# A two-layer decoder trunk on one core: halves of the convolution weights rounded behind copies of queries and probabilities, mixtures in the large pool's banks, and the order of roundings in the down projection

## The chip, the cores and the metric

One core of a Trainium2 chip runs the whole program. The metric is the device time of one execution in microseconds (us); of several runs the median is given. The engines are TensorE (PE, matrix products), VectorE (DVE), ScalarE (ACT), GpSimd (POOL) and SyncE (SP, here the issuer of nearly all DMAs). Each has its own queue of instructions and works through it in order.

## The reference, cut to what matters

512 tokens of width 1024 go through two layers. Layer 0 mixes by sliding-window attention beside a short gated convolution, layer 1 by a gated linear attention; each layer then has a gated feed-forward part with a convolution over time and a per-layer embedding gate.

```python
def _attn_conv_mixer(h, cos, sin, w_in, q_norm, k_norm, sinks, conv_w, w_out):
    b, s, _ = h.shape
    q, k, v, cb, cc, cx = _split(h @ w_in, HY_SPLITS)
    q = _apply_rope(_rms_norm(q.reshape(b, s, ATTN_Q_HEADS, HEAD_DIM), q_norm), cos, sin)
    k = _apply_rope(_rms_norm(k.reshape(b, s, ATTN_KV_HEADS, HEAD_DIM), k_norm), cos, sin)
    v = v.reshape(b, s, ATTN_KV_HEADS, HEAD_DIM)
    attn = _sliding_window_sink_attention(q, k, v, sinks)
    conv = cb * _causal_depthwise_conv(cc * cx, conv_w)
    return jnp.concatenate([attn, conv], axis=-1) @ w_out

def _conv_ffn(h, w_up, conv_w, conv_b, w_down):
    u = _causal_depthwise_conv(h @ w_up, conv_w) + conv_b
    gate, up = jnp.split(u, 2, axis=-1)
    return (jax.nn.gelu(gate, approximate=False) * up) @ w_down
...
    for i in range(DEPTH):
        j = i // 2
        h = _rms_norm(x, mix_norm[i])
        if i % 2 == 0:
            x = x + _attn_conv_mixer(h, cos, sin, hy_w_in[j], ...)
        else:
            x = x + _gla_mixer(h, gla_w_in[j], ...)
        x = x + _conv_ffn(_rms_norm(x, ffn_norm[i]), ffn_w_up[i], ffn_conv_w[i], ffn_conv_b[i], ffn_w_down[i])
        x = x + _per_layer_embedding(x, p[i], ple_norm[i], ple_w_gate[i], ple_w_proj[i])
```

The attention has 8 query heads of width 64 over 2 key heads, a window of 128 and four blocks of 128 queries. The down projection takes 2816 rows to 1024 columns.

## The kernel before, in words

**Numbers in two parts.** Every float32 operand of a large product is rounded to float32r (the high part) and the rest is kept as a second float32r tile (the low part). `cut` does it for weights: ScalarE copies `raw` to `wh` (L146), VectorE subtracts to get `wl` (L147), in pieces of 128x1024. `mm3` then makes three matmuls: high by high (L166), high by low (L167) and low by high (L168). `split` does the same for activations (L109 on ScalarE, L110 on VectorE). `weights` loads a piece of 1024 KB by SP into one of two `raw` buffers and cuts it.

**Banks.** TensorE writes to two pools of four banks each: `ps`, the large pool of this text, for the sums of long products, and `pa`, for transposes, scores and part products.

**The mixer of layer 0.** Queries, keys and values are made first. Then the four attention blocks run, between the products of the convolution: `conv_in` multiplies the tokens by 256 columns of the weights x, c or b, as two products of 24 matmuls of 128x512 each (the first with the first 128 columns, the second with the other 128), for two groups `j2` of columns. For a block `t`, `query` scales and turns the queries by position, `query_turned` transposes them on TensorE and copies them with ScalarE to `qT` (L547), `scores` makes query by key (L611, a `pa` bank for each pair), masks with VectorE and takes the exponentials with ScalarE, `probs` scales them (L652 on ScalarE), transposes them (L658) and copies them to `pT` (L664 on VectorE, L666 on ScalarE), and `mix` multiplies them by the values into one bank and splits the result to the operands `b0`, `b1` (L109, L110). The code writes these calls out in a fixed order, interleaved with `conv_w` (load and round 256 columns). Here a scheduler sets the order of the instructions on each engine, from that order and its own estimates; `tc.issue_after(x)` keeps an instruction behind `x`, which in the orders below shows only on the engine of that instruction.

**The down projection.** `down` goes through a list `plan` of 16 steps in the order written, for four units `u` of 256 columns. A step is a plain product (its matmuls are L166 to L168 into `ps`), and four of them have a fifth entry `s`, the number of a unit of 256x256 blocks that is multiplied with seven products instead of eight: `seven` (matmuls L886 to L888), a generator that is advanced by `next(g)` between the matmuls of the plain step. Its part sums are copied from bank to bank by ScalarE: L897, L907 and, last, L911 (`turned_over`), without which the next product in that bank can't go on. `cut_blocks` rounds a unit's weights (L833 on ScalarE, L834 on VectorE), and L857, L858 and L865 form differences of weight blocks on VectorE. `todo` lists the roundings of coming steps, and `pump(1)` issues what has come due. `settled(ends)` adds the finished banks of a unit to the residual `xT` (`add`, L1194) and starts the next norm (`finish`, whose squares and scaled copies are L276, L285 and L1321). TensorE's order in `down` is that of the code; the other engines' is the scheduler's.

```python
                    next(g)
                    cut_done(s)
                    pump(1)
                    steps(3, 4)
                    pump(1)
                    settled(ends)
```

Of the kernel before, what the change touches and what calls it, by code (L numbers as in the profile page):

```python
# [14 lines left out]
ALU = mybir.AluOpType  # L15
# [3 lines left out]
P = 128  # L19
# [3 lines left out]
ND = D // P  # L23
# [33 lines left out]
class Kernel:  # L57
# [369 lines left out]
    def mixer0(self):  # L427
        nc, a, tc = self.nc, self.a, self.tc
        with tc.tile_pool(name="m0", bufs=1) as mp:
            w_in = a["hy_w_in"][0].rearrange("(k p) n -> p k n", p=P)  # L430
# [111 lines left out]
            def turned(x, dst, copy):  # L542
                pst = self.pa()
                for g in range(4):
                    pairv = x[:, 2 * g : 2 * g + 2, :].rearrange("p a b -> p (a b)")
                    nc.tensor.transpose(pst[:, g * P : (g + 1) * P], pairv, self.ident)
                copy(dst, pst)  # L547


            kT = self.sp.tile([P, S], F32, tag="acc", name="kT", bufs=1)  # L550
# [38 lines left out]

            def query_turned(t, qn):  # L590
                qT = mp.tile([P, 4, P], F32, tag="qT", name=f"qT{t}", bufs=4)
                turned(qn, qT.rearrange("p a b -> p (a b)"), nc.scalar.copy)
                qTs.append(qT)

            ss, dens = {}, {}
            ya = [self.pair(self.fp, "b0", "b1") for _ in range(4)]

            def scores(t):
# [40 lines left out]
                nc.vector.reciprocal(den, den)  # L639
                ss[t], dens[t] = s, den  # L640

            pTs, copied = {}, {}

            def probs(t):

# [21 lines left out]

            def mix(t):

                po = self.pa()  # L670
                n = 2 if t else 1
                for g in range(2):
                    for c in range(n):
                        v = vs[t - 1 + c] if t else vs[0]
                        nc.tensor.matmul(
                            po[64 * g : 64 * g + 64, :], v[:, g * HD : (g + 1) * HD],
                            pTs[t][:, c, 4 * g : 4 * g + 4, :].rearrange("p a b -> p (a b)"),
                            start=c == 0, stop=c == n - 1,
                        )
                for j in range(4):  # L680
                    cols = slice(t * P, (t + 1) * P)
                    self.split((ya[j][0][:, cols], ya[j][1][:, cols]), po[:, j * P : (j + 1) * P])


            yc = [None] * 4
# [5 lines left out]
            def conv_w(nme, j2):  # L691
                c0 = starts[nme] + 256 * j2
                return self.weights(w_in[:, :, c0 : c0 + 256], ND, 256)

            def conv_in(nme, w):
                for c in range(2):
# [23 lines left out]
            def conv_out(j2, cs=(0, 1)):  # L720
                for c in cs:
                    xs, y = pre[c]
                    nc.vector.tensor_tensor(xs, pss["b", c], R, ALU.mult)
                    nc.vector.tensor_tensor(y, y, xs, ALU.mult)
                    hl = self.pair(self.fp, "b0", "b1")
                    self.split(hl, y)
                    yc[2 * j2 + c] = hl


            w = conv_w("x", 0)  # L730
# [11 lines left out]
            query_turned(1, qn1)  # L742
            scores(0)
            conv_in("c", w)
            w = conv_w("b", 0)
            conv_taps(0)
            qn3 = query(3)
            query_turned(2, qn2)
            probs(0)
            scores(1)  # L750
            conv_in("b", w)
            w = conv_w("x", 1)
            conv_out(0, (0,))
            query_turned(3, qn3)
            mix(0)
            probs(1)
            with tc.issue_after(copied[1, 0]):
                conv_out(0, (1,))
            scores(2)
            conv_in("x", w)  # L760
            w = conv_w("c", 1)
            mix(1)
            probs(2)
            scores(3)
            conv_in("c", w)
            w = conv_w("b", 1)
            conv_taps(1)
            mix(2)
            probs(3)
# [337 lines left out]
    def down(self, i, acts, forms, both, work, finish):  # L1107
# [83 lines left out]
                f()  # L1191

        def add(m, ps):
            nc.vector.tensor_tensor(self.xT[m], self.xT[m], ps, ALU.add)  # L1194

        due = [2 if u < blocked else 1 for u in range(4)]
        block_left = blocked
# [3 lines left out]
        with tc.manual_schedule(engines={ET.PE}):  # L1201
# [4 lines left out]
            for t, (u, name, k0, k1, s) in enumerate(plan):  # L1206
# [25 lines left out]
                if s is None:  # L1232
                    steps(0, k1 - k0)
                    settled(ends)
                    pump(1)
                    pend()
                    if work:
                        work.pop(0)()
                        if not work:
                            load_inner(inner.pop(0))  # L1240
                else:
                    g = gens[s]
                    steps(0, 1)
                    next(g)
                    steps(1, 2)
                    next(g)
                    steps(2, 3)
                    next(g)
                    cut_done(s)
                    pump(1)  # L1250
                    steps(3, 4)
                    pump(1)
                    settled(ends)
                    X, Y, V = next(g)
                    pump(1)
                    x = self.xT[2 * s + 1].rearrange("p (u t) -> p u t", u=2)
                    nc.vector.tensor_tensor(x, x, V.unsqueeze(1).to_broadcast([P, 2, H]), ALU.add)
                    if s == 3:
                        banks[3] = [X, Y]
                    else:  # L1260
                        add(2 * s, X)
                        add(2 * s + 1, Y)
                    pend()
                    due[s] -= 1
                    block_left -= 1
                    settled(False)
# [864 lines left out]
```

## Time and profile before

| | us |
|---|---|
| three runs, median (lowest to highest) | 1200.52 (1199.79 to 1200.64) |
| the profiled execution | 1201.93 |
| its span in the profile | 1200.1 |
| TensorE busy, in the span | 1191.8 |
| VectorE busy | 994.1 |
| ScalarE busy | 685.1 |

In the lines of a profile, a time stands first (us from the start of the span), then the duration, the engine, the line of the kernel, the operation, the tile that is written, an arrow and the tiles that are read, and the shape. "x16" is a group of sixteen such instructions on a row; the duration is then from the first's start to the last's end. In brackets stands the idle time of the engine before it and who ended it. A line of the list of waits has the waiting engine, tile and line, the engine, tile and line that released it, the sum of the waits, their count and the mean. Matmuls are pipelined, so their records overlap: how long one takes in a row is seen from the next one's start.

### The profile page before, as it was taken

To read this page: it belongs to the slowest core of one execution; us is meant where nothing else is said; L and a number is where in the kernel's file an instruction comes from. 1 tells how busy PE (TensorE), PEld (TensorE's weight loads), DVE (VectorE), ACT (ScalarE), POOL (GpSimd) and SP (SyncE) were. 2 spreads that over 40 slices of the span, in tenths; PEclk is the share of its full clock that TensorE was granted. 3 is DMA by queue.
4 is the path that set the end of the run, shared out by engine and by line. 5 is a ranking of instruction groups with operands and counts; after the bars stand their busy time and mean duration, and the time that the engine had idled before them with its cause. 6 is when DMAs were issued, how large, how long until landed. Compare 5 with 4: busy or idle time off the path is not lost.

```text
span 1200.1 us, 17976 instructions
## 1 busy us (share of the span) xinstructions
PE 1191.8 (99%) x7121; PEld 1038.1 (87%) x7121; DVE 994.1 (83%) x1571; ACT 685.1 (57%) x1116; POOL 43.0 (4%) x64
## 2 busy tenths in 40 slices
PE   9999999999999999999999999999999999999998
PEld 8877788999899889889988988889899999889887
DVE  6786587899999996779779876687999999986895
ACT  7566465556565744566563564555555656644764
POOL 2600000000000000000100000000000000000000
PEclk9999999999999999999999999999999999999999
DMA  7221322423233343331422222323242423423601
GB/s 223 86 91 38 97 80 70 127 85 118 94 101 111 106 141 97 97 106 61 149 59 70 71 71 70 106 64 112 71 141 71 134 79 119 136 88 97 211 1 70
DMA packets 110856, 117.62 MB, mean 98 GB/s; under 512 B 2824, under 2 KB 105794, under 8 KB 110772
## 3 DMA queue, kind: packets, MB, share of 16 engines
q1 hardware_dynamic: 109936, 115.88, 29.9%
q8 instruction: 56, 0.92, 0.3%
q0 software_dynamic: 560, 0.42, 0.3%
q14 instruction: 28, 0.23, 0.1%
q10 hardware_dynamic: 276, 0.18, 0.1%
HBM read 114.37 MB, written 2.10 MB: 97 GB/s over the span
## 4 chain that ended last, share of the span: by engine, by line
PE 89%; DVE 5%; ACT 2%; issue 1%; DMA 1%; POOL 1%; SPq 0%; DVEq 0%; ACTq 0%; POOLq 0%
PE ps L166 12%; PE ps L167 12%; PE ps L168 12%; PE pa L167 7%; PE pa L166 7%; PE pa L168 7%; PE ps L886 6%; PE ps L888 6%; PE ps L887 6%; PE pa L886 2%; PE pa L888 2%; PE pa L887 2%; PE ps L1496 1%; PE ps L1495 1%; PE ps L1494 1%
## 5 line engine op out<-in xcount | busy, mean ns | idle before, releaser
L146 ACT ACTIVATE wh<-raw 128x1024 fp32r<-128x1024 f32 (+4 forms) x144 | 143.6, 998 | 112.4 <-PE ps L167 64.8
L147 DVE TENSOR_TENSOR wl<-raw,wh 128x1024 fp32r<-128x1024 f32 (+4 forms) x144 | 165.8, 1152 | 29.9 <-ACT wh L146 29.0
L833 ACT ACTIVATE wh<-raw 128x1024 fp32r<-128x1024 f32 x84 | 89.2, 1062 | 120.6 <-DVE raw L858 65.1
L946 DVE SCALAR_TENSOR_TENSOR zt<-z,vfa,zt 128x510 f32<-128x510 f32 (+1 forms) x176 | 130.9, 746 | 5.3 <-ACT zt L944 4.7
L834 DVE TENSOR_TENSOR wl<-raw,wh 128x1024 fp32r<-128x1024 f32 x84 | 102.8, 1223 | 22.5 <-ACT wh L833 22.4
L944 ACT ACTIVATE zt<-z,vfb 128x512 f32<-128x512 f32 x88 | 71.1, 810 | 21.7 <-DVE four L997 8.3
L166 PE MATMUL ps<-b,wh 128*128 128x512 f32 x192 | 76.3, 397 | 0.0
L167 PE MATMUL ps<-b,wh 128*128 128x512 f32 x192 | 75.0, 390 | 0.0
L168 PE MATMUL ps<-b,wl 128*128 128x512 f32 x192 | 74.9, 390 | 0.0
L886 PE MATMUL ps<-four,wh 128*128 128x256 f32 x256 | 71.6, 280 | 0.7 <-ACT ps L911 0.7
L888 PE MATMUL ps<-four,wl 128*128 128x256 f32 x256 | 71.0, 277 | 0.0
L887 PE MATMUL ps<-four,wh 128*128 128x256 f32 x256 | 70.8, 277 | 0.0
L167 PE MATMUL pa<-b,wh 128*128 128x512 f32 x176 | 69.0, 392 | 0.0
L167 PE MATMUL pa<-a,wh 128*128 128x512 f32 x176 | 69.0, 392 | 0.0
L166 PE MATMUL pa<-a,wh 128*128 128x512 f32 x176 | 69.0, 392 | 0.0
L166 PE MATMUL pa<-b,wh 128*128 128x512 f32 x176 | 69.0, 392 | 0.0
L168 PE MATMUL pa<-b,wl 128*128 128x512 f32 x176 | 68.5, 389 | 0.0
L168 PE MATMUL pa<-a,wl 128*128 128x512 f32 x176 | 68.4, 389 | 0.0
L886 PEld LDWEIGHTS ps<-four,wh 128*128 128x128 f32 x256 | 48.0, 188 | 3.4 <-ACT ps L911 1.6
L166 PE MATMUL ps<-a,wh 128*128 128x512 f32 x128 | 50.6, 395 | 0.0
L166 PE MATMUL ps<-uh,wh 128*128 128x512 f32 x128 | 50.3, 393 | 0.0
L167 PE MATMUL ps<-ul,wh 128*128 128x512 f32 x128 | 50.1, 391 | 0.0
(496 smaller groups left out, 3597.1 us busy)
## 6 DMA issues: line engine op xcount, KB each, us to landing
raw<-in_ffn_w_up_dram SPq DMA_DIRECT2D x44, 1024.0 KB, 5.1
raw<-in_ffn_w_down_dram SPq DMA_DIRECT2D x12, 1024.0 KB, 5.1
raw<-in_hy_w_in_dram SPq DMA_DIRECT2D x8, 1024.0 KB, 5.1
raw<-in_gla_w_in_dram SPq DMA_DIRECT2D x8, 1024.0 KB, 5.2
raw<-in_ffn_w_down_dram SPq DMA_DIRECT2D x8, 768.0 KB, 4.4
raw<-in_ple_w_gate_dram SPq DMA_DIRECT2D x6, 1024.0 KB, 5.1
raw<-in_hy_w_out_dram SPq DMA_DIRECT2D x16, 256.0 KB, 4.1
zt<-in_ffn_w_down_dram SPq DMA_DIRECT2D x8, 512.0 KB, 3.7
```

Source lines behind the costliest of these rows:

```text
L146: nc.scalar.activation(hv, v, AF.Copy)
L147: self.rest = nc.vector.tensor_tensor(lv, v, hv.bitcast(F32), ALU.subtract)
L166: mm(out, lh, rh, start=start, stop=False, **kw)
L167: mm(out, lh, rl, start=False, stop=False, **kw)
L168: return mm(out, ll, rh, start=False, stop=stop, **kw)
L833: nc.scalar.activation(h, src, AF.Copy)
L834: nc.vector.tensor_tensor(l, src, h.bitcast(F32), ALU.subtract)
L886: mm(out, wh, xh, start=first and j == 0, stop=False, **kw)
L887: mm(out, wh, xl, start=False, stop=False, **kw)
L888: mm(out, wl, xh, start=False, stop=j == ND // 2 - 1, **kw)
L944: nc.scalar.activation(y, z, AF.Identity, scale=w2[:, f : f + 1], bias=bb[:, f : f + 1])
L946: nc.vector.scalar_tensor_tensor(out=y[:, tap:], in0=z[:, : S - tap], scalar=w[:, f : f + 1], in1=y[:, tap:], op0=ALU.mult, op1=ALU.add,)
```

## The change

Three things change.

1. In the mixer, `turned` returns its copy, and `copied["q", t]` holds that of `qT`. The weights b of the first group and x, c and b of the second are no longer rounded by `conv_w` but by `conv_halves`: the same load, and then the two halves of 128 columns each with a `cut` of its own, behind an instruction that is named: b's first half behind the copy of block 1's turned queries and its second behind the second ScalarE copy of block 0's probabilities; x's behind that and behind the last split of block 0's mixture; both of c's behind block 1's second ScalarE copy of probabilities; both of the last b's behind block 2's.
2. `mix` takes its bank from `ps`, not from `pa`.
3. In `down`, in the steps that have a seven-product unit, the last matmuls of the plain step and the additions (`settled`) come ahead of the two `pump(1)`, and what the first of these issues is kept behind L911 and, where a unit ended, behind the last addition.

```diff
@@ -544,7 +544,7 @@
-                copy(dst, pst)
+                return copy(dst, pst)
@@ -589,10 +589,10 @@
-                turned(qn, qT.rearrange("p a b -> p (a b)"), nc.scalar.copy)
+                copied["q", t] = turned(qn, qT.rearrange("p a b -> p (a b)"), nc.scalar.copy).ins
@@ -667,7 +667,7 @@
-                po = self.pa()
+                po = self.ps()
@@ -679,7 +679,8 @@
-                    self.split((ya[j][0][:, cols], ya[j][1][:, cols]), po[:, j * P : (j + 1) * P])
+                    last = self.split((ya[j][0][:, cols], ya[j][1][:, cols]), po[:, j * P : (j + 1) * P])
+                mixed[t] = last[1].ins
@@ -691,6 +692,20 @@
+            def conv_halves(nme, j2, ins):
+                c0 = starts[nme] + 256 * j2
+                raw = self.raw(ND, 256)
+                nc.sync.dma_start(raw, w_in[:, :, c0 : c0 + 256])
+                ws = []
+
+                def half(ins):
+                    c = slice(len(ws) * P, len(ws) * P + P)
+                    with tc.issue_after(ins):
+                        ws.append(self.cut(raw[:, :, c], "b"))
+
+                half(ins)
+                return (lambda k, a, b: ws[a // P](k, 0, P)), half
@@ -742,28 +757,32 @@
-            w = conv_w("b", 0)
+            w, second = conv_halves("b", 0, copied["q", 1])
             conv_taps(0)
             qn3 = query(3)
             query_turned(2, qn2)
             probs(0)
+            second(copied[0, 1])
             scores(1)
             conv_in("b", w)
-            w = conv_w("x", 1)
+            w, second = conv_halves("x", 1, copied[0, 1])
             conv_out(0, (0,))
             query_turned(3, qn3)
             mix(0)
             probs(1)
             with tc.issue_after(copied[1, 0]):
                 conv_out(0, (1,))
+            second(mixed[0])
             scores(2)
             conv_in("x", w)
-            w = conv_w("c", 1)
+            w, second = conv_halves("c", 1, copied[1, 1])
+            second(copied[1, 1])
             mix(1)
             probs(2)
             scores(3)
             conv_in("c", w)
-            w = conv_w("b", 1)
+            w, second = conv_halves("b", 1, copied[2, 1])
+            second(copied[2, 1])
@@ -1191,7 +1210,7 @@
-            nc.vector.tensor_tensor(self.xT[m], self.xT[m], ps, ALU.add)
+            self.added = nc.vector.tensor_tensor(self.xT[m], self.xT[m], ps, ALU.add)
@@ -1247,10 +1266,14 @@
                     cut_done(s)
+                    steps(3, 4)
+                    settled(ends)
+                    with ExitStack() as es:
+                        es.enter_context(tc.issue_after(self.turned_over.ins))
+                        if ends:
+                            es.enter_context(tc.issue_after(self.added.ins))
+                        pump(1)
                     pump(1)
-                    steps(3, 4)
-                    pump(1)
-                    settled(ends)
```

How the instructions move: line numbers of the changed kernel are larger by up to 23 (L833 becomes L852, L834 L853, L897 L916, L907 L926, L911 L930, L1194 L1213, L1321 L1344), and buffer numbers differ. First ScalarE around block 1's turned queries, before:

```order
L146 ACTIVATE wh_808<-raw_802 128x1024
L712 ACTIVATE cy_818<-pad_813,vec_104_682 128x512
L652 ACTIVATE s_713<-s_713,den_738 128x128 x4
L146 ACTIVATE wh_966<-raw_964 128x1024
L547 COPY qT_850<-pa_851 128x512
L666 COPY pT_862<-pa_863 128x512
L666 COPY pT_862<-pa_869 128x512
```

and after:

```order
L727 ACTIVATE cy_814<-pad_809,vec_104_682 128x512
L652 ACTIVATE s_713<-s_713,den_738 128x128 x4
L547 COPY qT_846<-pa_847 128x512
L666 COPY pT_858<-pa_859 128x512
L666 COPY pT_858<-pa_865 128x512
L727 ACTIVATE cy_824<-pad_819,vec_104_682 128x512
L146 ACTIVATE wh_871<-raw_802 128x1024
L146 ACTIVATE wh_966<-raw_964 128x1024
```

`raw_802` is the load of b and `raw_964` that of x. The second half of b and the first half of x moved from ahead of the copies of `qT` and `pT` to behind them. On VectorE in the next block, before:

```order
L724 TENSOR_TENSOR cy_828<-cy_828,cxs_822 128x512
L147 TENSOR_TENSOR wl_1126<-raw_1123,wh_1125 128x1024
L664 COPY pT_1003<-pa_1010 128x512
L110 TENSOR_TENSOR b_67_549<-pa_987,b_66_548 128x128
L664 COPY pT_1003<-pa_1022 128x512
L110 TENSOR_TENSOR b_69_551<-pa_987,b_68_550 128x128
```

and after:

```order
L739 TENSOR_TENSOR cy_824<-cy_824,cxs_818 128x512
L110 TENSOR_TENSOR b_67_549<-ps_983,b_66_548 128x128
L664 COPY pT_999<-pa_1006 128x512
L110 TENSOR_TENSOR b_69_551<-ps_983,b_68_550 128x128
L664 COPY pT_999<-pa_1018 128x512
```

The rest of c's weights (`raw_1123`) left this place for one behind the masking of the scores; the mixture's splits (L110) read a `ps` bank. On ScalarE in that block, x's second half (`wh_1030`) now stands where c's first half stood, ahead of `qT`, and c's first half comes after the copies of `pT`. Last, ScalarE in the first seven-product unit of layer 0's down projection, before:

```order
L907 COPY ps_4367<-ps_4368 128x256
L146 ACTIVATE wh_4451<-raw_4299 128x1024
L911 COPY ps_4368<-ps_4367 128x256
L109 ACTIVATE wh_4461<-zt_4271 128x4x128
L109 ACTIVATE wh_4461<-zt_4273 128x4x128
L833 ACTIVATE wh_4495<-zt_4271 128x1024
L276 ACTIVATE acc_4073<-xT_103 128x512
L1321 ACTIVATE sum_5118<-xT_103,vec_104_682 128x512
L897 COPY ps_4518<-pa_4516 128x256
```

and after:

```order
L926 COPY ps_4367<-ps_4368 128x256
L930 COPY ps_4368<-ps_4367 128x256
L146 ACTIVATE wh_4459<-raw_4299 128x1024
L109 ACTIVATE wh_4463<-zt_4271 128x4x128
L109 ACTIVATE wh_4463<-zt_4273 128x4x128
L276 ACTIVATE acc_4073<-xT_103 128x512
L1344 ACTIVATE sum_5118<-xT_103,vec_104_682 128x512
L852 ACTIVATE wh_4495<-zt_4271 128x1024
L916 COPY ps_4518<-pa_4516 128x256
```

The bank copy L911 goes ahead of the rounding L146, and the two norm instructions go ahead of the unit's rounding L833. VectorE at the same place has both additions L1194 of the finished unit ahead of L147, where one stood behind L857; and the first addition of the next unit ahead of L858, where it stood behind it. The orders of POOL and of SP's DMAs are unchanged.

More of the change, by code (lines that the diff above doesn't have):

```diff
@@ L591, in query_turned @@
                 qT = mp.tile([P, 4, P], F32, tag="qT", name=f"qT{t}", bufs=4)
-                turned(qn, qT.rearrange("p a b -> p (a b)"), nc.scalar.copy)
+                copied["q", t] = turned(qn, qT.rearrange("p a b -> p (a b)"), nc.scalar.copy).ins
                 qTs.append(qT)
-            ss, dens = {}, {}
+            ss, dens, copied, mixed = {}, {}, {}, {}
             ya = [self.pair(self.fp, "b0", "b1") for _ in range(4)]
@@ L640, in scores @@
                 ss[t], dens[t] = s, den
-            pTs, copied = {}, {}
+            pTs = {}
             def probs(t):
```

## The prediction

> **What bounds the kernel now.** I read the page's engine sums first, then the waits of TensorE, then the timeline of TensorE in the stretches that the diff touches, then ScalarE and VectorE in the same stretches.
>
> ```profile
> span 1200.1 us, 17976 instructions
> PE 1191.8 (99%) x7121; PEld 1038.1 (87%) x7121; DVE 994.1 (83%) x1571; ACT 685.1 (57%) x1116; POOL 43.0 (4%) x64
> PE ps L886 <- ACT ps L911: 0.7, 1, 0.7
> PE pa L611 <- DVE pT L664: 0.5, 1, 0.5
> PE pa L611 <- DVE b L110: 0.3, 1, 0.3
> ```
>
> PE is busy 1191.8 of 1200.1 us, and the diff takes no matmul away. It can only win back gaps between matmuls. The listed waits it could touch are 0.5 and 0.3 us; the 0.7 us one is in the feed-forward of layer 1, where nothing changes. Smaller stalls hide inside "busy", since a matmul's record is longer than its turn. So I measure the step from one start to the next.
>
> ```profile
> 45.11 0.39 PE L168 MATMUL ps<-a,wl 128*128 128x512 f32 x1
> 45.34 0.39 PE L166 MATMUL ps<-a,wh 128*128 128x512 f32 x1
> 69.66 1.39 PE L658 MATMUL pa<-cf,s 128*128 128x128 f32 x8
> 70.97 2.81 PE L611 MATMUL pa<-kT,qT 64*128 64x256 f32 x16
> 73.71 0.50 PE L166 MATMUL ps<-a,wh 128*128 128x512 f32 x1
> 88.02 0.47 PE L166 MATMUL ps<-a,wh 128*128 128x512 f32 x1
> 88.94 1.99 PE L611 MATMUL pa<-kT,qT 64*128 64x256 f32 x12 [0.45 <-DVE pT L664]
> 92.26 0.50 PE L167 MATMUL ps<-a,wh 128*128 128x512 f32 x1
> 105.02 1.99 PE L658 MATMUL pa<-cf,s 128*128 128x128 f32 x16
> 106.93 2.81 PE L611 MATMUL pa<-kT,qT 64*128 64x256 f32 x16
> 109.67 0.50 PE L166 MATMUL ps<-a,wh 128*128 128x512 f32 x1
> ```
>
> A free 128x512 matmul takes 0.23 us (45.11 to 45.34). Sixteen transposes of L658 take 1.91 us (105.02 to 106.93), so eight should take 0.95; in block 1 they took 1.31 (69.66 to 70.97): 0.36 lost. Twelve score matmuls of L611 have a record of 1.99 with the tail of the last, so sixteen should take 16/12 of 1.99 less its tail of some 0.29, so 2.27 us, an estimate; blocks 1 and 3 took 2.74 (70.97 to 73.71, 106.93 to 109.67): 0.47 lost in each. Block 2 lost 0.92 − 0.23 = 0.69 ahead of the scores (88.02 to 88.94) and 3.32 − 2.27 = 1.05 in them (88.94 to 92.26). Together 3.0 us: all that the attention part can bring.
>
> **Part 1, the roundings in the attention blocks.** Who keeps PE waiting there:
>
> ```profile
> 70.13 1.04 ACT L146 ACTIVATE wh<-raw 128x1024 fp32r<-128x1024 f32 x1
> 71.08 0.56 ACT L547 COPY qT<-pa 128x512 f32<-128x512 f32 x1
> 85.36 1.04 ACT L146 ACTIVATE wh<-raw 128x1024 fp32r<-128x1024 f32 x1
> 88.20 0.68 DVE L664 COPY pT<-pa 128x512 f32<-128x512 f32 x1
> 90.86 0.29 DVE L110 TENSOR_TENSOR b<-pa,b 128x128 fp32r<-128x128 f32 x1
> ```
>
> In block 1 the copy of the turned query (L547) starts at 71.08 because a weight rounding of 1.04 us from 70.13 stands ahead of it on ScalarE. The diff puts that rounding behind the copy, and the copy can start about 0.9 us sooner; the 0.36 + 0.47 = 0.83 lost here shrink by 0.7, I take, as a hand-over stays. In block 2 three things hold PE: the copy of the query behind a rounding (85.36), the copy of probabilities on VectorE (88.20, ending 88.88 just before the scores at 88.94), and a `pa` bank that the mixture's last split (90.86, ending 91.15) holds. The new bank pool removes the third, and the rounding's rest now goes behind the scores on VectorE. But x's second half is ordered by `mixed[0]`, a VectorE instruction, and ScalarE's rounding of it, 1.04 us, stands ahead of L547 in the new order as the old one did. So of 1.74 I take 0.3, what the profile's waits give the bank. In block 3 I take 0.3 of 0.47. Sum −1.3; ends 0 and −3.0.
>
> What the moved roundings cost: b's second half now comes behind the probabilities' copies, near 72.5 (from L547's end at 71.64, less 0.9, and three ScalarE copies near 0.6 each), and is ready 1.04 and some 1.2 us later, near 75. PE starts that product at 73.71 with the first half, 24 matmuls by 0.23 = 5.5 us, so it wants the second half at 79.2: 4 us of cover. The loads of the raw weights (1024 KB each, on SP's queue, in the same order) wait for a raw buffer that frees a few us later; the next product is another 24 matmuls away, so cover again. The mixture's bank out of `ps` takes one of four; a convolution's product asks for one only when it starts, and the split that frees it (90.86) is within 3 us. I cost all three at nothing; without cover each would be 1 to 2 us.
>
> **Part 2, the down projection.** In each of its three first seven-product units per layer, PE waits for the copy L911, and in the first one also for the addition of a finished unit:
>
> ```profile
> 453.35 0.39 PE L168 MATMUL ps<-uh,wl 128*128 128x512 f32 x1
> 453.71 0.39 PE L886 MATMUL ps<-a,wh 128*128 128x256 f32 x1
> 453.93 0.28 PE L887 MATMUL ps<-a,wh 128*128 128x256 f32 x1
> 454.05 0.28 PE L888 MATMUL ps<-a,wl 128*128 128x256 f32 x1
> 457.04 0.39 PE L168 MATMUL ps<-uh,wl 128*128 128x512 f32 x1
> 457.37 0.50 PE L166 MATMUL ps<-uh,wh 128*128 128x512 f32 x1
> ```
>
> The step 453.35 to 453.71 is 0.36, so 0.13 too long; the first matmul after a wait then takes 0.22 (to 453.93) where the next takes 0.12, another 0.10. So a stall is worth 0.23, six of them 1.4. At 457.04 the step to the matmul that waits for the addition is 0.33, 0.10 too long; with the same 0.10 behind it that is 0.2, twice 0.4. I take the other units and layer 1 as like these. Removed: −1.8 in all, as L911 now starts ahead of the rounding and both additions come first on VectorE.
>
> What it adds is lateness of the roundings:
>
> ```profile
> 452.32 1.06 ACT L146 ACTIVATE wh<-raw 128x1024 fp32r<-128x1024 f32 x1 [2.34 <-PE ps L887]
> 453.08 0.69 DVE L1194 TENSOR_TENSOR xT<-xT,ps 128x512 f32<-128x512 f32 x1 [2.56 <-PE ps L168]
> 453.69 1.22 DVE L147 TENSOR_TENSOR wl<-raw,wh 128x1024 fp32r<-128x1024 f32 x1
> 457.23 0.69 DVE L858 TENSOR_TENSOR zt<-zt,zt 128x512 f32<-128x512 f32 x1
> 458.01 1.06 ACT L833 ACTIVATE wh<-zt 128x1024 fp32r<-128x1024 f32 x1 [3.27 <-DVE zt L858]
> 458.97 0.61 ACT L276 ACTIVATE acc<-xT 128x512 f32<-128x512 f32 x1
> 459.49 0.71 ACT L1321 ACTIVATE sum<-xT,vec 128x512 f32<-128x512 f32 x1
> 459.10 1.23 DVE L834 TENSOR_TENSOR wl<-zt,wh 128x1024 fp32r<-128x1024 f32 x1
> 461.19 0.28 PE L888 MATMUL pa<-a,wl 128*128 128x256 f32 x1
> 475.14 1.23 DVE L834 TENSOR_TENSOR wl<-raw,wh 128x1024 fp32r<-128x1024 f32 x1 [1.19 <-ACT wh L833]
> 476.60 0.28 PE L888 MATMUL pa<-a,wl 128*128 128x256 f32 x1
> 1075.95 0.61 ACT L285 ACTIVATE acc<-xT 128x512 f32<-128x512 f32 x1
> ```
>
> One more addition, a turn of 0.61 (453.08 to 453.69), stands ahead of the chain L147, L858 on VectorE. L858 ends near 458.5 instead of 457.92. In that time two norm instructions, L276 and L1321, become ready and stand ahead of L833 on ScalarE in the new order (turns of 0.52 and some 0.6), so L833 starts 1.1 later, near 459.1, and L834, which now ends at 460.33, ends near 461.45. PE wants it at 461.19 less the 0.23 + 0.21 just won, 460.75. New wait 0.75, plus 0.10 on the first matmul: 0.85. The next small block of the same unit is rounded behind it, another 0.1. In the second unit L146 alone is later: 0.36, L911's turn, less 0.15 of slack that ScalarE had, so 0.2 at L834 (475.14, ending 476.37 against PE at 476.60, slack 0.23), and PE comes 0.23 sooner: wait 0.2 to 0.3, with 0.10 behind it 0.35. Third unit: no norm work and no added addition, nothing. Layer 0: 1.3. In layer 1 one norm instruction (L285, 0.61) instead of two stands ahead of L833, so the first wait is about 0.5 smaller, but the last unit's L911 gets a split of 512 columns, an estimated 0.6, ahead of it on ScalarE, a wait of 0.3 to 0.4 and 0.10 behind it: 1.3 again. Added +2.6; net of part 2 +0.8. Its ends: −1.8, if none of it shows, and +3.0, if the lateness of 1.1 us runs on through all three units of both layers less half of the slack.
>
> **A rule beside the rows.** The Trainium skill, "TensorE: Matmul & The Clock Gate", section "Architectural detail: the array is 16× 32×32, not 1× 128×128", says that PE's queue can pull a weight load ahead of matmuls in flight. By that rule a released matmul would find its weights loaded, and the 0.10 on the first matmul would be no part of the stall.
>
> ```profile
> 857.97 0.19 PEld L886 LDWEIGHTS ps<-four,wh 128*128 128x128 f32 x1 [1.16 <-ACT ps L911]
> ```
>
> This load starts only with the wait's end, 1.16 us idle before it, so the trace speaks for the other view here. By the rule the six stalls would bring 0.8 instead of 1.4, and the added ones would cost about 0.4 less; the sum moves by 0.2 us and no chance changes.
>
> **The sum.** −1.3 + 0.8 = −0.5 on the profiled execution of 1201.9 us, whose span is 1200.1 with 1.8 around it: 1201.4. That run lies 1.4 above the median of 1200.5; the same difference on the median gives **1200.0 us**.
>
> **Rivals.** (a) The new waits in the down projection do not arise, because the norm instructions finish in the gaps that ScalarE has before L858 ends: −1.3 − 1.8 = −3.1, 1197.4 us. For it: VectorE and ScalarE idle 2 to 3 us before most of these rows (2.34, 2.56, 3.27). Against: those idle stretches end just when the chain L146 to L834 begins, and its slack of 0.86 (460.33 to 461.19) is less than 1.1. Chance 0.10. (b) It ends slower. Place: first unit of each layer, on ScalarE, L276 and L1321 ahead of L833. Price: from a lateness of 0.86 on, all goes to PE; if `issue_after` of the additions holds the second rounding too, every unit starts its next one late by 1 us, six times less half for slack, +3.0, and if attention gives nothing either: 1203.5 us. For it: 475.14 shows a slack of only 0.23 in the second unit. Against: each unit also runs 24 plain matmuls on PE (by 0.23, 5.5 us), in which the roundings can catch up. Chance 0.08. (c) The change does not do what it says in block 2, since x's half stays ahead of the copy: attention −1.0, sum −0.2, 1200.3 us. It is inside "same".
>
> **How the numbers follow.** A measurement of this kernel can tell 0.2%, 2.4 us, from no change. My forecast with (c), no visible change: 0.82; (a), faster than 1198.1: 0.10; (b), slower than 1202.9: 0.08. The range: from −2.4 (attention −2.4 and part 2 at 0) to +1.6 (attention −0.9, part 2 at +2.5 for roundings that lie later than worked out), 1198.1 to 1202.1; about 0.2 lies outside.
>
> **What would show it.** Right: L547 in block 1 starts within 0.2 us of the last transpose; no wait of L611 for L110; the steps to L886 fall to 0.23 in the down projection; a new wait of L888 for L834 of 0.5 to 0.9 near 461 and a smaller one in the second unit. Wrong: PE waits in the attention halves of products for a late second half, or down's steps of L888 show no new wait, or block 2's 1.74 us is won whole.

## The result, and the profile after

| | us |
|---|---|
| the kernel before, median of 22 runs (lowest to highest) | 1200.64 (1199.79 to 1203.67) |
| the changed kernel, median of 22 runs | 1198.93 (1198.07 to 1199.52) |
| ratio, 95% interval | 0.9985 (0.9978 to 0.9991) |
| profiled execution of the changed kernel (its span) | 1199.04 (1197.2) |

The change gains 1.7 us, 0.15%: within the 0.2% that were called no change, but with an interval that lies below 1. The forecast was 1200.0, 0.5 us less than the 1200.52 known then. The page and TensorE's waits of the changed kernel:

```profile
span 1197.2 us, 17966 instructions
PE 1189.6 (99%) x7121; PEld 1039.0 (87%) x7121; DVE 994.0 (83%) x1571; ACT 684.0 (57%) x1116; POOL 42.9 (4%) x64
PE pa L907 <- DVE wl L853: 1.2, 4, 0.7
PE pa L462 <- ACT a L112: 0.2, 1, 0.2
PE pa L658 <- ACT qT L547: 0.2, 1, 0.2
PE ps L905 <- ACT ps L930: 0.2, 1, 0.2
```

The waits for L664 and L110 are gone, and so is the one of 0.7 us for the copy between banks, L911. New are four of L907 (L888 of before) for the roundings in the down projection, 1.2 us in all, one for that copy (now L930) in the last unit of layer 1, and one of the transposes L658 in block 2 for the copy of the turned query, ahead of which x's second half is rounded.

TensorE runs the same 7121 matmuls in nearly one order, so the two traces can be laid side by side, matmul by matmul: the difference between the times from one matmul to another says what a stretch won or lost. These four rows of the timeline are the start and the end of the stretch that holds blocks 1 to 3, first before:

```profile
65.82 0.39 PE L166 MATMUL ps<-a,wh 128*128 128x512 f32 x1
116.86 0.39 PE L167 MATMUL ps<-a,wh 128*128 128x512 f32 x1
```

and after:

```profile
65.53 0.39 PE L166 MATMUL ps<-a,wh 128*128 128x512 f32 x1
114.02 0.39 PE L167 MATMUL ps<-a,wh 128*128 128x512 f32 x1
```

The stretch took 51.04 us (116.86 less 65.82) and now takes 48.49, 2.55 less. Here are the attention's rows after the change, first TensorE and then ScalarE:

```profile
70.34 2.00 PE L611 MATMUL pa<-kT,qT 64*128 64x256 f32 x16
87.02 0.66 PE L658 MATMUL pa<-cf,s 128*128 128x128 f32 x4 [0.22 <-ACT qT L547]
87.66 2.44 PE L611 MATMUL pa<-kT,qT 64*128 64x256 f32 x16
104.93 2.00 PE L611 MATMUL pa<-kT,qT 64*128 64x256 f32 x16
...
85.45 1.05 ACT L146 ACTIVATE wh<-raw 128x1024 fp32r<-128x1024 f32 x1
86.40 0.57 ACT L547 COPY qT<-pa 128x512 f32<-128x512 f32 x1
```

The scores of blocks 1 and 3 take 2.00 us where they took 2.81. In block 2 a rounding still stands from 85.45 ahead of L547, and the transposes L658 wait for the bank that this copy frees.

In the down projection of layer 0, first unit (TensorE, ScalarE, VectorE, changed kernel):

```profile
450.71 0.28 PE L905 MATMUL ps<-a,wh 128*128 128x256 f32 x1
450.83 0.28 PE L906 MATMUL ps<-a,wh 128*128 128x256 f32 x1
457.72 0.28 PE L906 MATMUL pa<-a,wh 128*128 128x256 f32 x1
458.68 0.39 PE L907 MATMUL pa<-a,wl 128*128 128x256 f32 x1 [0.68 <-DVE wl L853]
458.90 0.28 PE L905 MATMUL pa<-a,wh 128*128 128x256 f32 x1
...
455.17 0.63 ACT L276 ACTIVATE acc<-xT 128x512 f32<-128x512 f32 x1 [3.22 <-DVE xT L1213]
455.71 0.71 ACT L1344 ACTIVATE sum<-xT,vec 128x512 f32<-128x512 f32 x1
456.32 1.04 ACT L852 ACTIVATE wh<-zt 128x1024 fp32r<-128x1024 f32 x1
...
455.05 0.68 DVE L877 TENSOR_TENSOR zt<-zt,zt 128x512 f32<-128x512 f32 x1
457.40 1.22 DVE L853 TENSOR_TENSOR wl<-zt,wh 128x1024 fp32r<-128x1024 f32 x1 [1.06 <-ACT wh L852]
```

The stall at the copy between banks is gone (450.71 to 450.83 is a free turn of 0.12). In its place L907 starts 0.96 after the matmul ahead of it, 0.84 too late, and the next matmul 0.22 behind L907, another 0.10.

A third difference I take for no effect of the change, since none of its lines is near. Before, ScalarE waited long for a weight load in the feed-forward of layer 1; after, it did not:

```profile
838.31 1.06 ACT L833 ACTIVATE wh<-raw 128x1024 fp32r<-128x1024 f32 x1 [1.67 <-DMA raw<-in_ffn_w_up_dram]
```

```profile
834.63 1.06 ACT L852 ACTIVATE wh<-raw 128x1024 fp32r<-128x1024 f32 x1 [0.33 <-DMA raw<-in_ffn_w_up_dram]
```

All that follows on that stretch came 1.2 us later in the profile of before, down to the 0.74 us wait for L911 that the prediction set aside. That execution took 1201.93 us, 1.3 over its kernel's median. So the spans differ by 2.9 us and the medians by 1.7.

The table gives, for each profiled kernel, how much longer each stretch was than in the profile of before, in us, worked out from the starts of the same matmuls (times of before: block 0 52.8 to 65.8, block 1 to 82.2, block 2 to 101.0, block 3 to 116.9; down projections 450.6 to 492.6 and 1068.1 to 1130.4; the late load's stretch 841.5 to 866.2). "Sum" leaves the load's stretch out; "median" is the kernel's median less that of the runs of before beside it. Each row comes from one profiled execution.

| kernel | block 0 | block 1 | block 2 | block 3 | down 0 | down 1 | sum | median | late load |
|---|---|---|---|---|---|---|---|---|---|
| changed | −0.18 | −1.15 | −0.54 | −0.86 | +0.52 | +0.62 | −1.6 | −1.7 | −1.23 |
| e1_attn | −0.18 | −1.15 | −0.53 | −0.86 | −0.06 | 0.00 | −2.8 | −3.1 | −1.23 |
| e2_down | 0.00 | +0.03 | −0.03 | −0.02 | +0.55 | +0.62 | +1.2 | +0.7 | −1.23 |
| e3_mix_pa | −0.18 | −1.15 | +0.89 | +0.95 | +0.55 | +0.58 | +1.6 | +1.9 | −0.39 |
| e4_mix_only | 0.00 | +0.03 | −1.21 | −0.86 | −0.10 | +0.01 | −2.1 | −2.1 | −1.23 |
| e5b_x_behind_pT | −0.18 | −1.15 | −0.89 | −0.86 | +0.48 | +0.55 | −2.1 | −2.3 | −0.69 |
| e6_turned_only | −0.18 | −1.15 | −0.56 | −0.86 | +0.06 | +0.59 | −2.1 | −2.2 | −1.23 |
| e7_no_added | −0.18 | −1.15 | −0.57 | −0.86 | +0.55 | +0.55 | −1.7 | −1.9 | −1.00 |
| e8_x_turned | −0.18 | −1.15 | −0.87 | −0.86 | +0.01 | +0.56 | −2.5 | −2.9 | −1.14 |
| e9_norm_behind | −0.18 | −1.15 | −0.51 | −0.86 | +0.02 | +0.52 | −2.2 | −2.8 | −1.23 |
| e10_all | −0.18 | −1.15 | −0.87 | −0.86 | +0.05 | +0.58 | −2.4 | −2.9 | −1.23 |
| e11_attn_x | −0.18 | −1.15 | −0.89 | −0.86 | −0.03 | +0.03 | −3.1 | −3.3 | −1.23 |
| e12_best | −0.18 | −1.15 | −0.89 | −0.86 | −0.29 | +0.28 | −3.1 | −3.0 | −1.02 |

A stretch that two kernels share comes out alike to 0.1 us, so the stretches settle what the medians, with intervals of about a us on either side, cannot. The last column follows ScalarE's wait for that load in the same profile: it is 1.67 us before, 1.40 in e3_mix_pa, 1.08 in e5b_x_behind_pT, 0.82 in e7_no_added and 0.33 in the changed kernel. It goes with the load, and none of the edits is near that place; how much it varies between executions of one kernel was not tried.

### The profile page after: what moved, and what is told of

The parts are those of the page before. It is cut to its first block, busy times and chain, and to the rows that moved or that the text cites. A ratio compares the mean times of both kernels' runs of the same rounds, so it can differ in the third digit from the quotient of the medians.

```text
span 1197.2 us, 17966 instructions
## 1 busy us (share of the span) xinstructions
PE 1189.6 (99%) x7121; PEld 1039.0 (87%) x7121; DVE 994.0 (83%) x1571; ACT 684.0 (57%) x1116; POOL 42.9 (4%) x64
## 4 chain that ended last, share of the span: by engine, by line
PE 89%; DVE 5%; ACT 3%; issue 2%; POOL 1%; DMA 0%; SPq 0%; DVEq 0%; ACTq 0%; POOLq 0%
PE ps L166 12%; PE ps L168 12%; PE ps L167 12%; PE pa L167 7%; PE pa L166 7%; PE pa L168 7%; PE ps L905 6%; PE ps L907 6%; PE ps L906 6%; PE pa L907 2%; PE pa L905 2%; PE pa L906 2%; PE ps L1519 1%; PE ps L1518 1%; PE ps L1517 1%
## 5 line engine op out<-in xcount | busy, mean ns | idle before, releaser
L146 ACT ACTIVATE wh<-raw 128x1024 fp32r<-128x1024 f32 (+4 forms) x144 | 143.4, 999 | 97.0 <-PE ps L167 59.3
L147 DVE TENSOR_TENSOR wl<-raw,wh 128x1024 fp32r<-128x1024 f32 (+4 forms) x144 | 165.7, 1151 | 28.6 <-ACT wh L146 27.7
L852 ACT ACTIVATE wh<-raw 128x1024 fp32r<-128x1024 f32 x84 | 89.3, 1063 | 121.6 <-DVE raw L877 65.4
L853 DVE TENSOR_TENSOR wl<-raw,wh 128x1024 fp32r<-128x1024 f32 x84 | 102.6, 1221 | 20.6 <-ACT wh L852 20.5
L907 PE MATMUL ps<-four,wl 128*128 128x256 f32 x256 | 71.1, 278 | 0.0
L166 PE MATMUL ps<-a,wh 128*128 128x512 f32 x128 | 50.6, 395 | 0.0
L167 PE MATMUL ps<-a,wh 128*128 128x512 f32 x128 | 50.0, 390 | 0.0
```

Source lines behind the costliest of these rows:

```text
L146: nc.scalar.activation(hv, v, AF.Copy)
L147: self.rest = nc.vector.tensor_tensor(lv, v, hv.bitcast(F32), ALU.subtract)
L166: mm(out, lh, rh, start=start, stop=False, **kw)
L167: mm(out, lh, rl, start=False, stop=False, **kw)
L852: nc.scalar.activation(h, src, AF.Copy)
L853: nc.vector.tensor_tensor(l, src, h.bitcast(F32), ALU.subtract)
```

## The experiments

Each was timed in five rounds beside the kernel before.

### The two parts alone

The attention part alone is the changed kernel with the old order in `down`:

```diff
                     cut_done(s)
-                    steps(3, 4)
-                    settled(ends)
-                    with ExitStack() as es:
-                        es.enter_context(tc.issue_after(self.turned_over.ins))
-                        if ends:
-                            es.enter_context(tc.issue_after(self.added.ins))
-                        pump(1)
                     pump(1)
+                    steps(3, 4)
+                    pump(1)
+                    settled(ends)
```

> Only the attention part of the change (halves behind the copies, mixtures in the large pool's banks); the down projection as before. Theory (the two parts add up, read from matched matmul starts of the two traces: attention -2.8 us, down projection +1.1 us): median 1197.9 us beside 1200.6 of before, ratio 0.9977; the stretch from block 0's scores to the end of block 3's scores about 2.8 us shorter. Rival (the attention stretch in the two traces owes a part to one execution's luck, and the down projection costs nothing): 1198.9, ratio 0.9986.

Measured: 1197.62, ratio 0.9973 (0.9962 to 0.9984). The down projection alone is the kernel before with these lines the other way round, and `self.added` recorded.

> Only the down projection's part of the change; the attention as before. Theory: slower by 1.1 us, 1201.7, ratio 1.0009, with the wait of L888's successor for the rounding of the inner blocks 0.6 to 0.8 us long in the first unit of layer 0. Rival (the moved copy and additions are a gain, as the stalls they remove are 1.8 us in all): 1199.5 or less, ratio 0.999.

Measured: 1201.41, ratio 1.0007 (0.9998 to 1.0016); the interval includes no change, but its two down projections are 0.55 and 0.62 us longer, as in the changed kernel. The theory held: the attention part wins 2.7 to 2.8 us, the down projection gives back 1.1 to 1.2, and the stretches don't act on one another.

### Bank or roundings

The changed kernel with the mixtures back in `pa`, and the kernel before with the mixtures in `ps` and nothing else:

```diff
-                po = self.ps()
+                po = self.pa()
```

> The changed kernel with the mixtures back in the small pool's banks. Theory (the moved roundings carry the attention part, the bank only block 2's third cause): slower than the changed kernel by 0.3 to 0.6 us, 1199.4, the loss all in block 2's scores. Rival (the bank carries it): slower by 1.5 us or more, 1200.4.

> The kernel before with the mixtures in the large pool's banks and nothing else. Theory: faster by 0.3 to 0.6 us, 1200.2, in block 2's scores alone. Rival (the bank carries the attention part): faster by 1.5 us or more, 1199.1.

Measured: 1202.63, ratio 1.0014 (1.0005 to 1.0023), and 1198.64, ratio 0.9982 (0.9973 to 0.9990). The theory fell in both, and the rival held. The one line of the bank wins 2.1 us by itself, more than the whole change. Without it the attention part is no gain at all: +0.5 us (−0.18 − 1.15 + 0.89 + 0.95). Block 2 shows that the bank stood behind both of its listed waits. These are the transposes of before (their scores start at 88.94 and the product behind them goes on at 92.26), and then transposes, scores and product with the bank alone:

```profile
86.27 1.99 PE L658 MATMUL pa<-cf,s 128*128 128x128 f32 x16
...
85.75 1.97 PE L658 MATMUL pa<-cf,s 128*128 128x128 f32 x16
87.65 2.73 PE L611 MATMUL pa<-kT,qT 64*128 64x256 f32 x16
90.31 0.50 PE L166 MATMUL ps<-a,wh 128*128 128x512 f32 x1
```

The scores start 1.90 after the transposes where they started 2.67 after them, and take 2.66 to the next product where they took 3.32 (one matmul of the product, at 88.02, stood between them before, so the block gains 1.21 and not the sum of both). The waits for L110 and for L664's copy are both gone from the list: two score matmuls now start ahead of that copy's end at 88.33 (87.65 and 87.97), and the third at 88.39.

Block 3 shows the same of a stall that no wait in the list names. ScalarE and VectorE do the same things there in the kernel before and with the bank alone. Before, these are the last two of the four splits on VectorE, which end at 108.56 in the middle of the scores (106.93 to 109.67); a score matmul that gets this bank starts behind them, at 108.62, 0.50 after the one ahead of it:

```profile
107.65 0.28 DVE L110 TENSOR_TENSOR b<-pa,b 128x128 fp32r<-128x128 f32 x1
108.27 0.29 DVE L110 TENSOR_TENSOR b<-pa,b 128x128 fp32r<-128x128 f32 x1 [0.34 <-ACT b L109]
```

With the bank alone, TensorE and then VectorE:

```profile
105.19 2.00 PE L611 MATMUL pa<-kT,qT 64*128 64x256 f32 x16
...
105.91 0.28 DVE L110 TENSOR_TENSOR b<-ps,b 128x128 fp32r<-128x128 f32 x1
106.53 0.29 DVE L110 TENSOR_TENSOR b<-ps,b 128x128 fp32r<-128x128 f32 x1 [0.34 <-ACT b L109]
```

The splits come as late against the scores as before (the last one starts 1.34 after the scores' start in both, 106.93 to 108.27 and 105.19 to 106.53), but the scores no longer ask for the bank that they hold, and take 2.00 us, not 2.81. With the roundings moved and the bank not, ScalarE, VectorE and TensorE in the same place:

```profile
106.52 1.06 ACT L146 ACTIVATE wh<-raw 128x1024 fp32r<-128x1024 f32 x1
...
107.61 1.23 DVE L147 TENSOR_TENSOR wl<-raw,wh 128x1024 fp32r<-128x1024 f32 x1 [0.42 <-ACT wh L146]
109.38 0.29 DVE L110 TENSOR_TENSOR b<-pa,b 128x128 fp32r<-128x128 f32 x1
...
109.72 1.13 PE L611 MATMUL pa<-kT,qT 64*128 64x256 f32 x4 [0.44 <-DVE b L110]
```

Now the rounding that used to stand ahead of the copies stands between the mixture's splits, the last of which starts at 109.38, 2.99 us after the scores' start (106.39) instead of 1.34, and holds the `pa` bank that long. So the moved roundings need the bank here. In blocks 0 and 1 the roundings win 1.33 without it (the rows of e3_mix_pa and of the changed kernel agree); in block 2 they cost 0.67 beside it (−0.54 against −1.21), and in block 3 nothing.

### What is left of block 2

```diff
-            second(mixed[0])
+            second(copied[1, 1])
```

> The changed kernel with the rounding of x's second half behind the second ScalarE copy of block 1's probabilities instead of the mixture's last split. Theory (that rounding, 1.04 us on ScalarE ahead of the copy of block 3's turned queries, is what is left of block 2's loss: the transposes wait for the bank that this copy frees): faster than the changed kernel by 0.6 to 1.2 us, 1198.0, with no wait of the transposes for L547. Rival (the loss moves to the convolution's product, whose second half comes late, or to the scores): no gain, 1198.9.

Measured: 1198.57, ratio 0.9981 (0.9972 to 0.9990). The place was right, the size was not: block 2 wins a further 0.35 us, where 0.6 to 1.2 were expected. In its rows the sixteen transposes run through without the wait for L547, but take 2.41 us, where before they took 1.99, and the scores start 2.35 after the transposes, where in block 3 before it was 1.91 (105.02 to 106.93):

```profile
84.35 2.41 PE L658 MATMUL pa<-cf,s 128*128 128x128 f32 x16
86.70 2.61 PE L611 MATMUL pa<-kT,qT 64*128 64x256 f32 x16
...
84.98 0.57 ACT L547 COPY qT<-pa 128x512 f32<-128x512 f32 x1
```

L547 starts at 84.98, when the four scalings of block 1's probabilities ahead of it on ScalarE have ended. Only the bank alone, with the old order, comes to −1.21; which instruction the remaining 0.3 us go to was not tried.

### The price in the down projection

Three variants of the same edit follow. In the first, only the bank copy goes ahead of the rounding, and the additions stay where they were:

```diff
                     cut_done(s)
-                    steps(3, 4)
-                    settled(ends)
-                    with ExitStack() as es:
-                        es.enter_context(tc.issue_after(self.turned_over.ins))
-                        if ends:
-                            es.enter_context(tc.issue_after(self.added.ins))
-                        pump(1)
+                    with tc.issue_after(self.turned_over.ins):
+                        pump(1)
+                    steps(3, 4)
                     pump(1)
+                    settled(ends)
```

> The changed kernel, but in the down projection only the copy between banks goes ahead of the rounding; the additions and the last matmuls of the step stay where they were before. Theory (the additions first, and with them the norm instructions ahead of the inner rounding, cost 0.9 in layer 0 and 0.5 in layer 1 and bring 0.2 each): faster than the changed kernel by about 1.1 us, 1197.8; no wait near 0.8 in the first unit, the waits of 0.33 in the second units still there. Rival (the rounding behind the copy is itself the cost): no more than 0.4 faster, 1198.5, with the first unit's wait still there.

Measured: 1198.71, ratio 0.9981 (0.9972 to 0.9990), 0.2 below the changed kernel and not the expected 1.1; the stretches say 0.46 in layer 0 and nothing in layer 1. The first unit's wait for the rounding did go, as the theory had it. In its place the wait for the addition, 0.10 in layer 0 and 0.13 in layer 1 before, grew to 0.48 in each, with the same 0.10 behind it (TensorE, ScalarE and VectorE of this kernel):

```profile
453.96 0.50 PE L166 MATMUL ps<-uh,wh 128*128 128x512 f32 x1 [0.32 <-DVE xT L1213]
...
449.18 1.07 ACT L146 ACTIVATE wh<-raw 128x1024 fp32r<-128x1024 f32 x1
450.27 1.23 DVE L147 TENSOR_TENSOR wl<-raw,wh 128x1024 fp32r<-128x1024 f32 x1
453.22 0.68 DVE L1213 TENSOR_TENSOR xT<-xT,ps 128x512 f32<-128x512 f32 x1
```

VectorE's chain from L147 to the second addition waits for ScalarE's L146, which the copy has pushed back. In the second variant the additions come ahead, but nothing is kept behind the last of them (the two lines with `self.added.ins` left out):

> The changed kernel without the order behind the last addition; the additions are still written ahead of the roundings. Theory (the norm instructions ahead of the inner rounding on ScalarE are the price, and they stay there): as the changed kernel, 1198.9 within 0.4 us. Rival (holding the rounding behind the additions is the price): faster by about 0.8 us, 1198.1.

Measured: 1198.98, ratio 0.9983 (0.9974 to 0.9992), the stretches as in the changed kernel: it is the place of the additions and not that constraint. The third variant keeps the norm's square and scaled copy behind the rounding on ScalarE. Its lines stand where the blocks are rounded, in `down` and in the gate's sums:

```diff
+        rounded = nc.scalar.activation(h, src, AF.Copy)
+        if wide:
+            self.rounded = rounded
...
+                    with ExitStack() as es:
+                        if s == 0:
+                            self.inner = self.rounded
+                        if not block_left:
+                            es.enter_context(tc.issue_after(self.inner.ins))
+                        settled(False)
...
+                with tc.issue_after(self.inner.ins):
+                    nc.scalar.activation(rows[u], self.xT[m], AF.Copy, scale=self.g_ple[0][:, m : m + 1])
```

> The changed kernel with the norm's square and scaled copy of the first finished column kept behind the rounding of the inner blocks on ScalarE in the down projections; VectorE's and TensorE's orders as in the changed kernel. Theory (those two instructions ahead of the rounding are the price of the first unit's wait, 0.84 + 0.10 in layer 0 and 0.37 + 0.10 in layer 1; the addition that VectorE takes earlier leaves 0.1 to 0.2): faster than the changed kernel by 1.1 to 1.4 us, 1197.7. Rival (the earlier additions on VectorE are the price): the waits shrink by less than half, at most 0.5 us faster, 1198.5.

Measured: 1198.03, ratio 0.9980 (0.9971 to 0.9989). Theory and rival were both half right. L852 now starts as soon as VectorE's difference has ended, and TensorE's wait is 0.37 and 0.10 instead of 0.84 and 0.10 (ScalarE, then TensorE):

```profile
456.27 1.06 ACT L852 ACTIVATE wh<-zt 128x1024 fp32r<-128x1024 f32 x1 [3.88 <-DVE zt L879]
457.80 0.63 ACT L276 ACTIVATE acc<-xT 128x512 f32<-128x512 f32 x1
...
458.65 0.39 PE L909 MATMUL pa<-a,wl 128*128 128x256 f32 x1 [0.21 <-DVE wl L855]
```

So of layer 0's 0.94, 0.47 belongs to the two norm instructions and as much to VectorE's earlier additions behind a later L146. In layer 1 moving L285 changed nothing: the wait is 0.37 + 0.10 with it and without it, and is VectorE's alone.

### Put together

First the later place of x's second half and the bank copy alone in the down projection:

> Both together: x's second half behind block 1's copies of probabilities, and in the down projection only the copy ahead of the rounding. Theory (separate places, they add up): 1.9 us faster than the changed kernel, 1197.0, ratio 0.997 to the kernel before. Rival: no faster than the attention part alone, 1197.6.

Measured: 1198.01, ratio 0.9976 (0.9967 to 0.9985). Next the later norm instructions (e9_norm_behind) with the later place of x's second half:

> The same, and x's second half behind block 1's copies of probabilities. Theory: a further 0.4 us, 1197.3. Rival: no faster than the attention part alone, 1197.6.

Measured: 1197.99, ratio 0.9978 (0.9969 to 0.9987). The stretches add up in both (0.3 us in block 2 and 0.5 in layer 0's down projection against the changed kernel), but the theories asked for 1197.0 and 1197.3: the rivals held, and neither beats the attention part alone. The best attention part with the old down projection:

> The attention part with x's second half behind block 1's copies of probabilities, and the down projection as before the change. Theory: 0.4 us faster than the attention part alone, 1197.2, and within 0.4 us of the version with the down projection's norm instructions moved. Rival (the moved half's gain is luck of one execution): 1197.6.

Measured: 1197.58, ratio 0.9974 (0.9964 to 0.9984). By the medians this is the rival's number, no faster than the attention part alone (0.9973); the 0.36 us less in block 2 show in the stretches alone. The last run puts the copy ahead of the rounding in the third unit only (`if s == 2` ahead of the constraint, the old order otherwise):

> The attention part with x's second half behind block 1's copies of probabilities; the down projection as before the change, except that in its third seven-product unit alone the copy between banks goes ahead of the rounding. Theory (in that unit the removed stall of 0.23 us has no price, in the first two it has): 0.5 us faster than the same kernel with the down projection as before, 1197.1, ratio 0.997 to the kernel before, and each down projection 0.23 us shorter in the trace. Rival (the later rounding makes the next unit wait there too): no gain, 1197.6.

Measured: 1197.83, ratio 0.9974 (0.9964 to 0.9985). Each third unit is 0.25 us shorter, as expected. In layer 1 the fourth unit then waits 0.36 + 0.10, so the rival held there, and the median gained nothing. These are its ScalarE rows at that place:

```profile
1109.55 0.63 ACT L288 ACTIVATE sq<-xT 128x512 f32<-128x512 f32 x1 [0.55 <-DVE acc L289]
1111.44 0.36 ACT L930 COPY ps<-ps 128x256 f32<-128x256 f32 x1
```

and the same in the changed kernel:

```profile
1111.67 0.63 ACT L288 ACTIVATE sq<-xT 128x512 f32<-128x512 f32 x1 [0.55 <-DVE acc L289]
1113.56 0.36 ACT L930 COPY ps<-ps 128x256 f32<-128x256 f32 x1
```

In both, a norm square waits 0.55 us on VectorE in ScalarE's queue, and the bank copy behind it comes late.

## Why the prediction was right, and where it was not

**Direction and range** held: 1198.93 lies in 1198.1 to 1202.1, faster by less than 0.2%. The size did not: −1.7 us where −0.5 was forecast. The range held with some luck: attention's −2.7 lies beyond the −2.4 that its lower end allowed for, and the down projection's +1.1 brought the sum back inside.

**The step that failed** is the sum of part 1: "The new bank pool removes the third [...] So of 1.74 I take 0.3, what the profile's waits give the bank. In block 3 I take 0.3 of 0.47." Attention brought −2.7, not −1.3, and the bank alone −2.1 of it (1.21 in block 2, 0.86 in block 3). Three things were wrong. In block 2 the wait for L664's copy was taken as a cause that the bank would leave; with the bank alone that wait was gone as well. The list of waits names a releaser only where TensorE stood still between records; the stalls between matmuls whose records overlap it does not show, and in block 3 it showed none of 0.86. And the yardstick was itself stalled: "sixteen should take 16/12 of 1.99 less its tail" came from twelve matmuls of block 2, where the free scores take 2.00 with their tail (70.34, 104.93), so the 0.47 lost in blocks 1 and 3 was 0.8, and the end of −3.0 was too near.

The mechanism, once seen, is one of banks. The Trainium skill, "PSUM — Partial Sum Buffer", section "PSUM bank collisions raise a hardware error", has the rule to guard PSUM by bank and quadrant and not by address. The trace shows what such a guard costs here: a bank three of whose four parts had been read kept TensorE out until the fourth split, 108.27 to 108.56, had ended, and the score matmul started at 108.62. No run here shows what an access without that order would do.

**Block 1** brought 1.15 where 0.7 was taken. The cause was as told (roundings ahead of L547), but the loss of 0.83 was too low by the same yardstick, and the copy starts 1.2 us sooner and not 0.9: 0.63 after the transposes of its queries start (68.94 to 69.57) instead of 1.86 (69.22 to 71.08). **Block 2** went in part as the third rival had it: the moved roundings cost 0.67 beside the bank, and x's second half ahead of the copy has 0.35 of that.

**The down projection** was right in kind and near in size: +1.1 against +0.8. The first unit's new wait was put at 0.75 + 0.10 and came at 0.84 + 0.10; the second unit's 0.35 came at 0.33 + 0.10 (both layers); the last unit's in layer 1, 0.3 to 0.4 and 0.10, at 0.37 + 0.11. Three reasons behind it were off: half of the first wait is VectorE's and not the norm instructions'; layer 1's first wait was 0.47, not 0.35, and L285 has no part in it; and the last unit's wait came without the split ahead of L911 too (e12), from the square that waits in ScalarE's queue. The rival that the new waits don't arise is out (e2), and so is the slow one: no unit handed its lateness on.

**The first matmul behind a stall.** The sum took 0.10 us for it, against the rule on early weight loads in the Trainium skill, "TensorE: Matmul & The Clock Gate", section "Architectural detail: the array is 16× 32×32, not 1× 128×128". The runs bear the 0.10 out: it left with each stall (450.71 to 450.83 is 0.12) and came with each new one (458.68 to 458.90 is 0.22). What the rule would have changed was summed too low: the two removed waits for an addition also have 0.10 behind them, so the forecast would have moved by 0.4 us and not 0.2.

**What was costed at nothing** in part 1, the later second halves, the loads and the `ps` bank, cost nothing that shows: no wait for a late half or a late load of the convolution's weights stands among TensorE's waits after, and from start to start no step in the convolution's products of blocks 1 to 3 grew by more than 0.04 us.

## What to carry to other kernels

When a bank holds a result that four small instructions read, ask which later writer gets that bank, and move the result to a pool whose next writer is far off before moving the readers: here that one line won more than the whole change, and moving other work without it lost. On an engine that is 99% busy, measure stalls from start to start against a free stretch of the same matmuls, and make sure that the yardstick is free. An edit that moves an instruction ahead in an in-order queue to remove a wait of 0.13 us pays by what it pushes back in that queue: here the removals in the down projection together cost 1.1 us more than they won, while the third unit's alone won 0.25 us in layer 0. So try each removal alone.

## What was not expected of the hardware

One weight load of 1024 KB made ScalarE wait 1.67 us in the profiled execution of the kernel before, 1.40 in that of e3_mix_pa and 0.33 in that of the changed kernel, at the same place with the same work ahead, though none of the edits touches that place. The longest wait lengthened its execution by 1.2 us, nearly as much as the change. The start varies as well: up to the 25th matmul the profiled executions differ by up to 1.3 us.
